# Twelve of sixteen gate blocks as seven half-size products in a hybrid attention layer

## The chip, the core and the metric

The kernel runs on one core of one Trainium2 chip. The metric is device time in microseconds. A time is that of a whole execution; the profile's span is the part of it between the first and the last instruction that the profiler records.

In the profile PE is TensorE's matmul row and PEld its weight loads, DVE is VectorE, ACT is ScalarE, POOL is GpSimd, SP is SyncE, whose queue here issues the loads of weights. ps and pt are the names of the eight PSUM banks, four of each.

## The reference

One layer with D = 1024 and 512 tokens, with 16 meta tokens in front: a SwiGLU FFN, a token mixer and a second SwiGLU FFN, each added to the residual.

```python
h = h + 0.5 * swiglu(rms_norm(h, ffn1_norm[l]), ffn1_w_in[l], ffn1_w_out[l])
h = h + token_mixer(rms_norm(h, mix_norm[l]), ...)
h = h + 0.5 * swiglu(rms_norm(h, ffn2_norm[l]), ffn2_w_in[l], ffn2_w_out[l])
```

The change is in the mixer's second half, behind the two attentions (fox with 8 heads, SWA with 8 query heads on 2 key heads):

```python
proj = h @ w_in                                   # q, k, v of both branches, and the gates ga, gb
y = jax.nn.sigmoid(ga) * (o_fox @ w_branch_fox) + jax.nn.sigmoid(gb) * (o_swa @ w_branch_swa)
return y @ w_out
```

ga and gb have 1024 features each, o_fox and o_swa 512, y and the result 1024.

## The kernel before

**Numbers and products.** All large products run in fp32r with both operands split into a high part (a rounded copy, made by `hi` on ScalarE) and a low part (the rest, made by `lo` on VectorE). `prod` (L279, L280, L282) issues three matmuls for each pair of 128x128 weights and moving columns: wh with xH, wh with xL, wl with xH. So every weight piece costs one cast on ScalarE (L130, tile wh) and one subtraction on VectorE (L137, tile wl).

**Weights.** They come in pieces in the fixed order of the list `pieces`. `piece()` hands out the next one, splits three pieces ahead and loads five ahead. raw, wh and wl have three buffers each. An instruction waits in its engine's queue for the ones before it; which order the instructions of an engine have is set by a scheduler when the kernel is built, from the data they need, and does not change at run time.

**Seven products for eight.** The FFNs take two weight blocks and two token halves as a 2x2 block product and form it from seven half-size products (`Units.seven`): pieces A, B, C and D hold the blocks b1 and b2 and sums of their halves, the moving side is x in quarters (A11, A12, A22) and four sums of quarters (S1 to S4). The weight sums are made partly by accumulating loads that POOL issues (`load_first`, `load_others`) and partly by VectorE (L221, L222). Each product is 12 matmuls of half the tokens. One unit is 84 matmuls. The product of S4 (`p3`) is left pending and runs inside the next unit.

**The mixer.** Features lie on partitions, tokens on columns. x~ is the residual times the norm's gain, not yet times each token's rms factor (rb1); its two parts xH and xL are kept in SBUF. The residual is written to DRAM as h1d. After the two attentions' projections, four lists of steps are woven: attention units in `main` and plain products in `fills`, so that TensorE has matmuls while VectorE and ScalarE do a unit's softmax. An SWA unit is scores, turn (transposes of the weights) and values. The eight blocks of ga are such fills: four beside the first SWA head group, four beside the second. `keep_gate` stores each, times rb1, in zA. The gate stage follows: for each of four pairs of features two blocks of gb (24 matmuls of 512 columns each, from xH and xL), the sigmoids, then four branch products (12 matmuls each) with the split outputs oH, oL, and y split into yH, yL. The output projection takes token halves of 256 and adds into h2T, which is loaded from h1d on ScalarE's queue (L1516). Weight pieces of it follow each other every 24 matmuls.

Of the kernel before, what the change touches and what calls it, by code (L numbers as in the profile page):

```python
# [24 lines left out]
M = 16  # L25
# [11 lines left out]
NU = DFF // P  # L37
NC = (4, 3)
TH = T // 2

# [39 lines left out]
def kernel(  # L80
# [108 lines left out]
    xm_place = lambda n: cp.tile([P, KD * P], F32R, tag="xm", name=nm(n))  # L189
    state = {"use": 0, "load": 0, "split": 0}  # L190
    shared = {}
# [35 lines left out]
    def load_to(n):  # L227
        while state["load"] < min(n, len(pieces)):
            c = state["load"]
# [913 lines left out]
    def normalise(parts):  # L1143

        l = new("l", [P, 4], F32, 2)[:, : len(parts)]
        for j, (t, nmx) in enumerate(parts):
            A.activation(t, t, AF.Exp, bias=nmx, scale=-1.0, accum_out=l[:, j : j + 1])  # L1147
# [226 lines left out]

    def feat_steps(wsrc, srcH, srcL, nk, c0, use, cuts=4, w=S):

        box = {}

        def part(j):
            if j == 0:  # L1380
                box["w"] = wsrc()
                box["ps"] = psum()
# [42 lines left out]
    def pre(p, ip):  # L1425
# [33 lines left out]
    run(main[0][:1] + fills[0][:2])  # L1459
    del main[0][:1], fills[0][:2]  # L1460
    for m, f in zip(main, fills):
        run(weave(m, f))
    stM.close()


    stG = ExitStack()
    gp = stG.enter_context(tc.tile_pool(name="gates", bufs=1))
    yH = gp.tile([P, KD, S], F32R, name="yH")
    yL = gp.tile([P, KD, S], F32R, name="yL")
    oH = gp.tile([P, 2, 4, S], F32R, name="oH")  # L1470
    oL = gp.tile([P, 2, 4, S], F32R, name="oL")

    for c in range(4):
        sA, sB = {}, {}

        def gate_b(m):
            def use(ps):
                z = gp.tile([P, S], F32, tag="gz", name=nm("gz"), bufs=3)
                V.tensor_tensor(out=z, in0=ps, in1=rb1, op=ALU.mult)
                sB[m] = gp.tile([P, S], F32, tag="sg", name=nm("sg"), bufs=3)  # L1480
                A.activation(sB[m], z, AF.Sigmoid)

            return use

        for m in range(2):
            run(feat_steps(piece, xH, xL, KD, M, gate_b(m)))
        for m in range(2):
            sA[m] = gp.tile([P, S], F32, tag="sa", name=nm("sa"), bufs=3)
            A.activation(sA[m], zA[:, 2 * c + m], AF.Sigmoid)
        if c == 0:  # L1490
            for b in range(2):
                for k in range(4):
                    hi(oH[:, b, k], oA[:, b, k])
                    lo(oL[:, b, k], oA[:, b, k], oH[:, b, k])
        wF, wS = piece(), piece()
        for m in range(2):
            mi = 2 * c + m
            cut = lambda w: tuple(t[:, :, m * P : m * P + P] for t in w)

            def use_f(ps):  # L1500
                V.tensor_tensor(out=sA[m], in0=sA[m], in1=ps, op=ALU.mult)

            def use_s(ps):
                s = sB[m]
                V.tensor_tensor(out=s, in0=s, in1=ps, op=ALU.mult)
                V.tensor_tensor(out=s, in0=s, in1=sA[m], op=ALU.add)
                hi(yH[:, mi], s)
                lo(yL[:, mi], s, yH[:, mi])

            run(feat_steps(lambda: cut(wF), oH[:, 0], oL[:, 0], 4, 0, use_f))  # L1510
            run(feat_steps(lambda: cut(wS), oH[:, 1], oL[:, 1], 4, 0, use_s))

# [6 lines left out]
    def add_out(mi, c):  # L1519
        def use(ps):  # L1520
# [4 lines left out]
            else:  # L1525
                sq = gp.tile([P, S], F32, tag="gz", name=nm("sq2"), bufs=3)[:, : S // 2]
                A.activation(sq, hv, AF.Square)
# [178 lines left out]
```

## Time and profile before

| | |
|---|---|
| median of 3 runs | 1094.58 us (1093.43 to 1096.65) |
| profiled execution | 1096.85 us, span 1095.1 us, TensorE clock 0.996 |
| busy share | PE 99%, PEld 95%, DVE 76%, ACT 55%, POOL 15% |
| SWA units and fills | about 540 to 612 us |
| gate stage | 612 to 700 us |
| output projection | 700 to 747 us |

The lines of groups give out<-in by the program's names with shapes, then busy time and mean duration in ns. In a timeline a row is start, duration (both us), engine, line, operation, and in brackets how long the engine had been idle and what released it. A duration of TensorE, VectorE or ScalarE can overlap the next one's start.

### The profile page before, as it was taken

Reading aid. Unit: us, or ns where it says so; the run is one execution under the profiler, and the core shown is the slowest. Engines: PE = TensorE matmul, PEld = TensorE weight load, DVE = VectorE, ACT = ScalarE, POOL = GpSimd, SP = SyncE. Lnnn points to the kernel's source line nnn. Section 1 sums busy time; section 2 is a strip of 40 time slices with the busy share of each in tenths; the row PEclk is TensorE's granted clock in tenths of the full one; section 3 lists DMA queues with packets and bytes.
Section 4 is the critical chain, followed back from the end, with each engine's and each line's share of the span. In section 5 each row is a group of like instructions: output and inputs, shape, how many; then the busy total and the mean of one; then the engine's idle time right before and its main releaser. Section 6 shows DMA issues by size and latency. Waiting matters only on the chain.

```text
span 1095.1 us, 21329 instructions
## 1 busy us (share of the span) xinstructions
PE 1084.8 (99%) x8317; PEld 1036.0 (95%) x8317; DVE 831.5 (76%) x1569; ACT 600.8 (55%) x1115; POOL 167.4 (15%) x201
## 2 busy tenths in 40 slices
PE   9999999999999999999999999999999999999998
PEld 8999999999999999999887888899999999999997
DVE  6868868988889587788787655678798778886653
ACT  6556446656666455466555533355476466645640
POOL 1011111121124431122100000000122211221000
PEclk8999999999999999999999999999999999999999
DMA  8467787688776323112211224456589777887522
GB/s 272 114 196 192 174 197 199 153 221 211 178 179 170 119 88 109 59 40 80 79 58 58 77 86 147 153 174 182 136 192 185 193 192 178 180 192 181 147 77 78
DMA packets 96693, 161.45 MB, mean 147 GB/s; under 512 B 10112, under 2 KB 46464, under 8 KB 96592
## 3 DMA queue, kind: packets, MB, share of 16 engines
q1 hardware_dynamic: 65520, 119.93, 34.4%
q0 software_dynamic: 22688, 29.44, 18.1%
q10 hardware_dynamic: 8384, 10.72, 3.1%
q8 instruction: 65, 1.06, 0.4%
q14 instruction: 36, 0.29, 0.1%
HBM read 155.84 MB, written 6.32 MB: 148 GB/s over the span
## 4 chain that ended last, share of the span: by engine, by line
PE 95%; DVE 2%; ACT 1%; DMA 0%; issue 0%; POOL 0%; SPq 0%; ACTq 0%
PE ps L279 16%; PE ps L280 16%; PE ps L282 16%; PE pt L279 13%; PE pt L280 13%; PE pt L282 13%; ACT t L1147 1%; PE pt L1232 0%; DMA xt<-in_x_dram 0%; DVE wl L137 0%; PE pt L1187 0%; PE ps L1354 0%; PE pt L1354 0%; PE ps L1187 0%; DVE t L1150 0%; PE pt L1247 0%
## 5 line engine op out<-in xcount | busy, mean ns | idle before, releaser
L279 PE MATMUL ps<-x,wh 128*128 128x264 f32 (+2 forms) x768 | 226.4, 295 | 1.5 <-ACT pt L500 1.5
L280 PE MATMUL ps<-x,wh 128*128 128x264 f32 (+2 forms) x768 | 225.7, 294 | 0.9 <-DVE x L137 0.6
L282 PE MATMUL ps<-x,wl 128*128 128x264 f32 (+2 forms) x768 | 225.4, 294 | 0.0
L137 DVE TENSOR_TENSOR wl<-raw,wh 128x1024 fp32r<-128x1024 f32 (+3 forms) x136 | 164.5, 1210 | 75.6 <-ACT wh L130 73.5
L130 ACT CAST wh<-raw 128x1024 fp32r<-128x1024 f32 (+3 forms) x136 | 140.7, 1036 | 142.1 <-PE ps L280 46.7
L279 PEld LDWEIGHTS ps<-x,wh 128*128 128x128 f32 x768 | 145.9, 190 | 4.7 <-ACT pt L500 1.7
L280 PEld LDWEIGHTS ps<-x,wh 128*128 128x128 f32 x768 | 145.6, 190 | 3.9 <-DVE x L137 0.8
L282 PEld LDWEIGHTS ps<-x,wl 128*128 128x128 f32 x768 | 145.8, 190 | 2.8
L279 PE MATMUL pt<-x,wh 128*128 128x264 f32 (+2 forms) x416 | 125.4, 301 | 0.0
L280 PE MATMUL pt<-x,wh 128*128 128x264 f32 (+2 forms) x416 | 124.8, 300 | 0.0
L282 PE MATMUL pt<-x,wl 128*128 128x264 f32 (+2 forms) x416 | 124.6, 300 | 0.0
L137 DVE TENSOR_TENSOR wl<-tc,wh 128x1024 fp32r<-128x1024 f32 (+1 forms) x57 | 68.7, 1204 | 32.7 <-ACT wh L130 32.4
L130 ACT CAST wh<-tc 128x1024 fp32r<-128x1024 f32 (+1 forms) x57 | 59.0, 1035 | 58.2 <-DVE tc L222 48.3
L279 PE MATMUL ps<-acts,wh 128*128 128x264 f32 (+1 forms) x304 | 86.5, 285 | 0.0
L282 PE MATMUL ps<-acts,wl 128*128 128x264 f32 (+1 forms) x304 | 86.2, 283 | 0.0
L280 PE MATMUL ps<-acts,wh 128*128 128x264 f32 (+1 forms) x304 | 86.0, 283 | 0.0
L279 PEld LDWEIGHTS pt<-x,wh 128*128 128x128 f32 x416 | 78.4, 188 | 2.9 <-issue 0.3
L282 PEld LDWEIGHTS pt<-x,wl 128*128 128x128 f32 x416 | 78.5, 189 | 2.8
L280 PEld LDWEIGHTS pt<-x,wh 128*128 128x128 f32 x416 | 78.2, 188 | 2.5
L137 DVE TENSOR_TENSOR wl<-rawC,wh 128x1024 fp32r<-128x1024 f32 (+1 forms) x57 | 69.4, 1218 | 5.3 <-ACT wh L130 5.0
L130 ACT CAST wh<-rawC 128x1024 fp32r<-128x1024 f32 (+1 forms) x57 | 58.9, 1033 | 22.2 <-PE pt L280 15.7
L279 PE MATMUL pt<-acts,wh 128*128 128x264 f32 (+1 forms) x208 | 59.2, 285 | 0.0
(382 smaller groups left out, 3046.6 us busy)
## 6 DMA issues: line engine op xcount, KB each, us to landing
rawC<-in_w2i_dram SPq DMA_DIRECT2D x19, 512.0 KB, 4.4
raw<-in_w2i_dram SPq DMA_DIRECT2D x38, 256.0 KB, 3.7
rawC<-in_w1i_dram SPq DMA_DIRECT2D x18, 512.0 KB, 4.4
raw<-in_w1i_dram SPq DMA_DIRECT2D x36, 256.0 KB, 3.4
raw<-in_wm_dram SPq DMA_DIRECT2D x18, 512.0 KB, 4.5
raw<-in_wg_dram SPq DMA_DIRECT2D x16, 512.0 KB, 3.3
raw<-in_wout_dram SPq DMA_DIRECT2D x16, 512.0 KB, 3.3
rawD<-in_w2i_dram SPq DMA_DIRECT2D x19, 256.0 KB, 4.0
```

The costliest lines, as they stand in the source:

```text
L130: return A.copy(o, i)
L137: return V.tensor_tensor(out=o, in0=i, in1=h, op=ALU.subtract)
L279: PE.matmul(ps, sH, mH, start=first, stop=False, **more)
L280: PE.matmul(ps, sH, mL, start=False, stop=False, **more)
L282: shared["mm"] = PE.matmul(ps, sL, mH, start=False, stop=last, **more)
L1147: A.activation(t, t, AF.Exp, bias=nmx, scale=-1.0, accum_out=l[:, j : j + 1])
```

## The change

Sixteen gate blocks were plain products. Now the blocks 0 to 3 of ga stay plain and the other twelve (4 to 7 of ga, 0 to 7 of gb) go in six pairs through `Units.seven`, with token halves of 256. The order of the work around them changes:

- The fills beside the first SWA group are three gate blocks in place of four; beside the second they are the eight fox branch products, whose split inputs are written into buffers that earlier attention parts held (`fox_parts`), and whose results ScalarE copies out.
- The fourth gate block and the eight SWA branch products run after the attentions. The high parts of the SWA output go into a part of xH and xL that is not read any more (`Unused`), once the first half of that gate's matmuls is done.
- x~ in fp32 is made again, from h1d: four loads of 512 KB on ScalarE's queue, eight scalings on ScalarE (L1573), and on VectorE four sums of quarters (L1580), each then split (S1 to S4).
- Then six units: two for ga, in which POOL multiplies each sigmoid into the fox product (zA), and four for gb, in which VectorE multiplies the sigmoid into the SWA product, POOL adds zA, and y is split in pieces of 256 columns.
- The loads of the first unit's pieces B to D are held back until the gate stage's pool is open.

```diff
-    for m in range(KD):
-        pieces.append(("w", [(wg[m], 8, 128)]))
-    for c in range(4):
-        pieces += [("w", [(wg[KD + 2 * c + m], 8, 128)]) for m in range(2)]
-        pieces += [("w", [(wbr[b, c], 4, 256)]) for b in range(2)]
+    pieces += [("w", [(wg[m], 8, 128)]) for m in range(NG - 1)]
+    pieces += [("w", [(wbr[0, c], 4, 256)]) for c in range(4)]
+    pieces.append(("w", [(wg[NG - 1], 8, 128)]))
+    pieces += [("w", [(wbr[1, c], 4, 256)]) for c in range(4)]
+
+    hold = len(pieces) + 1
+    for m in range(NG, 2 * KD, 2):
+        seven_pieces(wg[m], wg[m + 1], 4)
...
-    gates = [s for m in range(KD) for s in feat_steps(piece, xH, xL, KD, M, keep_gate(m))]
+    gates = [s for m in range(NG - 1) for s in feat_steps(piece, xH, xL, KD, M, keep_gate(m))]
...
+    def split_o(b, oh_, ol):
+        for k in range(4):
+            src, l = oA[:, b, k], ol[:, k]
+            if b:
+                src, l = (v.rearrange("p (a c) -> p a c", a=2) for v in (src, l))
+            hi(oh_[:, k], src)
+            lo(l, src, oh_[:, k])
+
+    def fox_parts():
+
+        oF["h"] = new("v", [P, NB + 1, 512])[:, :4]
+        oF["l"] = new("qH", [P, 4, S])
+        oF["f"] = [new("k" + x, [P, 2, KW]).rearrange("p a c -> p (a c)").bitcast(F32) for x in "HL"]
+        split_o(0, oF["h"], oF["l"])
...
-        qb1[4:-1] + gates[:LAG] + qb1[-1:] + gates[LAG : 2 * KD],
-        gates[2 * KD :],
+        qb1[4:-1] + gates[:LAG] + qb1[-1:] + gates[LAG:],
+        foxes,
...
+    for k in range(0, KD, 2):
+        A.dma_start(xg[:, k : k + 2], h1d[:, k : k + 2])
...
+    def last_gate(ps):
+        V.tensor_tensor(out=zl, in0=ps, in1=rb1, op=ALU.mult)
+        A.activation(zl, zl, AF.Sigmoid)
+        V.tensor_tensor(out=zA[:, NG - 1], in0=zA[:, NG - 1], in1=zl, op=ALU.mult)
+
+    steps = feat_steps(piece, xH, xL, KD, M, last_gate, whole=True)
+    run(steps[:2])
+    split_o(1, oW, oLs)
+    run(steps[2:])
+    for k in range(KD):
+        A.activation(xg[:, k], xg[:, k], AF.Identity, scale=gmT[:, k : k + 1])
...
+    sum_of(0, xq(0, 0), xq(1, 0))
+    parts_of(0, "S3")
+    sum_of(1, xq(1, 0), xq(1, 1))
+    sum_of(2, at[1], xq(0, 0))
+    parts_of(2, "S2")
+    parts_of(1, "S1")
+    sum_of(3, xq(0, 1), at[2], ALU.add)
+    parts_of(3, "S4")
...
+    for m in range(KD):
+        run(branch_steps(1, m, (oW, oLs), lambda ps, m=m: A.copy(swa_out(m), ps)))
...
+        def sigma(i, t, v, in_place):
+            z = v if in_place else small("gz", 2)
+            tt(z, v, rb1[:, halves[t]])
+            c, mi = halves[t], m + i
+            sg = small("sg", 2)
+            A.activation(sg, z, AF.Sigmoid)
+            if b:
+                s = swa_out(mi)[:, c]
+                tt(s, s, sg)
+                (V if mi == KD - 1 and not t else G).tensor_tensor(out=s, in0=s, in1=zA[:, mi, c], op=ALU.add)
+                hi(yH[:, mi, c], s)
+                lo(yL[:, mi, c], s, yH[:, mi, c])
+            else:
+                G.tensor_tensor(out=zA[:, mi, c], in0=zA[:, mi, c], in1=sg, op=ALU.mult)
...
+            if what == "P7":
+                box["p7"] = small("p7")
+                A.copy(box["p7"], ps)
...
+            elif what == "C21 - U2":
+                u2 = small("u2")
+                A.copy(u2, box["u2"])
+                tt(u2, ps, u2, ALU.add)
+                sigma(0, 1, u2, True)
+            elif what == "C11":
+                sigma(0, 0, ps, False)
+            elif what == "C22 + P7":
+                o = small("c22")
+                tt(o, ps, box["p7"], ALU.subtract)
+                sigma(1, 1, o, True)
+            else:
+                sigma(1, 0, ps, False)
...
+    for m in range(NG, KD, 2):
+        gg.seven(gate(m, 0), False, src)
+    for m in range(0, KD, 2):
+        gg.seven(gate(m, 1), m == KD - 2, src)
```

Three places in VectorE's order show it. The first is the entry into the gate stage. Before, from the last attention output (oA) on: the low parts of the attention outputs (oL) stand between the first gate's z (gz) and weight pieces (wl).

```order
L1061 TENSOR_TENSOR oA<-pt_8178,hsq_8188 64x2x128
L1398 TENSOR_TENSOR zA<-pt_8138,rb_4863 128x512
L137 TENSOR_TENSOR wl_8213<-raw_8028,wh_8212 128x1024
L137 TENSOR_TENSOR oL<-oA,oH 128x512 x4
L1479 TENSOR_TENSOR gz_8243<-ps_8218,rb_4863 128x512
L137 TENSOR_TENSOR oL<-oA,oH 128x512
L137 TENSOR_TENSOR wl_8248<-raw_8136,wh_8247 128x1024
```

Now (spare is the z of the last plain gate and then the place of the x~ sums, oLs the low parts of the SWA output, x_42.. its high parts, xg x~, S_1397 the sum S3, S_1389 S1, S_1398 S2, wl_8286 the third piece of the SWA branch):

```order
L1564 TENSOR_TENSOR spare<-pt_8229,rb_4863 128x512
L138 TENSOR_TENSOR oLs<-oA,x_4275 128x512
L138 TENSOR_TENSOR oLs<-oA,x_4276 128x512
L138 TENSOR_TENSOR oLs<-oA,x_4279 128x512
L138 TENSOR_TENSOR oLs<-oA,x_4280 128x512
L1566 TENSOR_TENSOR zA<-zA,spare 128x512
L1580 TENSOR_TENSOR spare<-xg 128x1024 x2
L138 TENSOR_TENSOR S_1397_8215<-spare,S_1397_8215 128x1024
L1580 TENSOR_TENSOR spare<-spare,xg 128x1024
L138 TENSOR_TENSOR S_1389_8203<-spare,S_1389_8203 128x1024
L1580 TENSOR_TENSOR spare<-xg,spare 128x1024
L138 TENSOR_TENSOR S_1398_8217<-spare,S_1398_8217 128x1024
```

The next row is L138's wl_8286: the weight piece stands behind the x~ sums and three of their low parts.

The second place is the middle of the stage. Before, one pair of features between two weight pieces (sa and sg the sigmoids of ga and gb, then the products):

```order
L1501 TENSOR_TENSOR sa_8594<-sa_8594,ps_8610 128x512
L1505 TENSOR_TENSOR sg_8557<-sg_8557,pt_8624 128x512
L1506 TENSOR_TENSOR sg_8557<-sg_8557,sa_8594 128x512
L137 TENSOR_TENSOR yL<-sg_8557,yH 128x512
L1501 TENSOR_TENSOR sa_8596<-sa_8596,ps_8641 128x512
L137 TENSOR_TENSOR wl_8605<-raw_8563,wh_8604 128x1024
```

Now, a part of the second unit of gb (oA holds the SWA product and becomes y, sg is the sigmoid, u and c the gate's z in place):

```order
L138 TENSOR_TENSOR wD_8903<-rawD_8753,wD_8903 128x512
L225 TENSOR_TENSOR tc_8992<-rawC_8906,rawD_8907 128x512
L1611 TENSOR_TENSOR oA<-oA,sg_8897 128x256
L1611 TENSOR_TENSOR u_1507_8937<-ps_8868,u_1507_8937 128x256
L226 TENSOR_TENSOR tc_8992<-tc_8992,rawC_8906 128x512
L138 TENSOR_TENSOR yL<-oA,yH 128x256
L1611 TENSOR_TENSOR u_1507_8937<-u_1507_8937,rb_4863 128x256
L1611 TENSOR_TENSOR gz_8963<-pt_8854,rb_4863 128x256
L138 TENSOR_TENSOR wl_8996<-tc_8992,wh_8995 128x1024
L1611 TENSOR_TENSOR oA<-oA,sg_8941 128x256
L1611 TENSOR_TENSOR oA<-oA,sg_8965 128x256
```

The operations on y are half as wide and twice as many, and weight sums and more splits stand between them.

The third place is the start of the output projection. Before, the sums into h2T and the splits of its weight pieces alternate:

```order
L137 TENSOR_TENSOR yL<-sg_8740,yH 128x512
L1522 TENSOR_TENSOR h2T<-h2T,ps_8837 128x256
L137 TENSOR_TENSOR wl_8865<-raw_8756,wh_8864 128x1024
L1522 TENSOR_TENSOR h2T<-h2T,pt_8870 128x256
L137 TENSOR_TENSOR wl_8900<-raw_8835,wh_8899 128x1024
```

Now (wl_9368 is the fourth piece of the output projection):

```order
L1625 TENSOR_TENSOR oA<-oA,zA 128x256
L138 TENSOR_TENSOR yL<-oA,yH 128x256
L1668 TENSOR_TENSOR h2T<-h2T,pt_9340 128x256
L1668 TENSOR_TENSOR h2T<-h2T,ps_9373 128x256
L1668 TENSOR_TENSOR h2T<-h2T,pt_9408 128x256
L138 TENSOR_TENSOR wl_9368<-raw_9297,wh_9367 128x1024
L1674 TENSOR_TENSOR sqacc<-sqacc,gz_9399 128x256
```

Three sums into h2T stand ahead of the piece.

More of the change, by code (lines that the diff above doesn't have):

```diff
@@ L38 @@
 NC = (4, 3)
+NG = 4
 TH = T // 2
@@ L189 @@
     xm_place = lambda n: cp.tile([P, KD * P], F32R, tag="xm", name=nm(n))
-    state = {"use": 0, "load": 0, "split": 0}
+    state = {"use": 0, "load": 0, "split": 0, "hold": hold}
     shared = {}
@@ L227, in load_to @@
     def load_to(n):
-        while state["load"] < min(n, len(pieces)):
+        while state["load"] < min(n, state.get("hold", n), len(pieces)):
             c = state["load"]
@@ L1460 @@
     del main[0][:1], fills[0][:2]
+    main[3].insert(0, fox_parts)
     for m, f in zip(main, fills):
         run(weave(m, f))
+    for m in range(NG - 1):
+        with after(shared["exp"]):
+            A.activation(zA[:, m], zA[:, m], AF.Sigmoid)
+        V.tensor_tensor(out=zA[:, m], in0=zA[:, m], in1=fox_out(m), op=ALU.mult)
     stM.close()
@@ L1467 @@
     gp = stG.enter_context(tc.tile_pool(name="gates", bufs=1))
[L1468 to L1511, printed above, removed]
@@ new lines @@
+    HF = S // 2
+    halves = (slice(0, HF), slice(HF, S))
+    shared["tp"] = gp
+    shared["wd"] = lambda: xm_place("wD")
+    banks["turn"] = None
+    spare = gp.tile([P, KD, S], F32, tag="yL", name="spare")
+    part = lambda name: gp.tile([P, 2, 4, HF], F32R, tag=name, name=nm(name))
+    small = lambda tag, bufs=1: gp.tile([P, HF], F32, tag=tag, name=nm(tag), bufs=bufs)
+    xS = {"S1": part("S1")}
+    oLs = gp.tile([P, 4, S], F32R, name="oLs")
+    for tag, n in (("p7", 1), ("gz", 2), ("sg", 2), ("u2", 1), ("c22", 1)):
+        for _ in range(n):
+            small(tag, n)
@@ new lines @@
+    gp.tile([P, PW], F32, tag="tc", name="tc", bufs=1)
+    for _ in range(2):
+        gp.tile([P, 512], F32, tag="rawD", name="rawD", bufs=2)
+    xS["S3"] = part("S3")
+    xg = gp.tile([P, KD, S], F32, tag="yH", name="xg")
+    for name in ("S2", "S4"):
+        xS[name] = part(name)
+    del state["hold"]
+    for k in range(0, KD, 2):
+        A.dma_start(xg[:, k : k + 2], h1d[:, k : k + 2])
+    zl = spare[:, KD - 1]
+    def last_gate(ps):
+        V.tensor_tensor(out=zl, in0=ps, in1=rb1, op=ALU.mult)
+        A.activation(zl, zl, AF.Sigmoid)
+        V.tensor_tensor(out=zA[:, NG - 1], in0=zA[:, NG - 1], in1=zl, op=ALU.mult)
```

58 lines of the change are left out of this document (54 added, 4 removed).

## The prediction, made before the result was known

> **What bounds the kernel now.** I read the page's first part, then the stretches of the stages that the change touches, then the single instructions there.
>
> ```profile
> PE 1084.8 (99%) x8317; PEld 1036.0 (95%) x8317; DVE 831.5 (76%) x1569; ACT 600.8 (55%) x1115; POOL 167.4 (15%) x201
> ...
> 612.00:700.00 88.00, 88.00 (x382) 71.64 (x381) 49.45 (x62) 33.37 (x47) 0.00 (x0) 1.00 0.35 114
> ...
> 700.00:747.00 47.00, 47.00 (x395) 46.81 (x394) 37.32 (x59) 24.29 (x34) 0.70 (x1) 1.00 0.54 180
> ...
> 800.00:850.00 50.00, 50.00 (x424) 49.96 (x423) 44.48 (x77) 32.00 (x58) 11.64 (x10) 1.00 0.89 196
> ```
>
> The columns of a stretch are its length, then busy time and instructions of PE, PEld, DVE, ACT and POOL. TensorE is never idle in the gate stage (612 to 700), in the output projection behind it, or in the second FFN's seven-product units. In the gate stage DVE is busy for 49 of 88 us and POOL does nothing; in the FFN units DVE is at 44 of 50. So the gate stage costs what its matmuls cost, and has room on DVE that seven-product units use up.
>
> A matmul's listed duration overlaps its neighbours; its cost is the distance between starts.
>
> ```profile
> L279 PE MATMUL ps<-oH,wh x32: 389/389/401, 622.3 to 696.6; 128*128 128x512 f32 x32
> ...
> 806.62 0.28 PE L279 MATMUL pt<-x,wD 128*128 128x256 f32 x1
> ...
> 816.55 0.28 PE L279 MATMUL pt<-x,wD 128*128 128x256 f32 x1
> ```
>
> The first row's first and last instruction are 321 matmuls apart in program order: 74.3 / 321 = 0.2315 us for one of 512 columns. The other two are the same place in two successive units, 84 matmuls of 256 columns: 9.93 us, 0.118 each.
>
> **The change, part by part.**
>
> *Fewer columns.* A pair of gate blocks takes 2 x 24 = 48 matmuls of 512 columns, 11.11 us; as a unit it takes 9.93. Six pairs: 6 x 1.18 = **-7.1 us**. The branch products keep their 192 matmuls; four gates stay plain. SWA's second head group keeps its fill (96 matmuls of branch product for 96 of gates); the first gives up 24, which run later and alone. The shortest cover left between scores and their transposes there is 18 matmuls, 4.2 us, as in pieces of the order before, where TensorE never waited: 0, at worst +1.
>
> *The DVE's price list.*
>
> ```profile
> 800.06 0.68 DVE L137 TENSOR_TENSOR wD<-rawD,wD 128x512 fp32r<-128x512 f32 x1
> 800.66 0.42 DVE L794 TENSOR_TENSOR sums<-u,sums 128x256 f32<-128x256 f32 x1
> ...
> 801.59 0.42 DVE L137 TENSOR_TENSOR acts<-sums,acts 128x256 fp32r<-128x256 f32 x1
> 801.93 0.42 DVE L537 TENSOR_TENSOR u<-ps,u 128x256 f32<-128x256 f32 x1
> 802.26 0.68 DVE L221 TENSOR_TENSOR tc<-rawC,rawD 128x512 f32<-128x512 f32 x1
> 802.98 0.69 DVE L222 TENSOR_TENSOR tc<-tc,rawC 128x512 f32<-128x512 f32 x1
> ...
> 804.87 1.22 DVE L137 TENSOR_TENSOR wl<-tc,wh 128x1024 fp32r<-128x1024 f32 x1
> 806.01 1.22 DVE L137 TENSOR_TENSOR wl<-rawC,wh 128x1024 fp32r<-128x1024 f32 x1
> ...
> 816.79 0.43 DVE L794 TENSOR_TENSOR sums<-u,u 128x256 f32<-128x256 f32 x1
> 817.25 0.43 DVE L794 TENSOR_TENSOR sums<-sums,u 128x256 f32<-128x256 f32 x1
> ```
>
> Start to start: 1024 columns 1.14 us, 512 columns 0.60, 256 columns 0.335; behind an operation that makes its input 0.72 and 0.46.
>
> *Entry of the stage.* DVE now makes the kept gate's z (0.60) before the four low parts of the SWA output. TensorE's second branch matmul needs the first of them, about 0.60 + 0.68 + hand-over = 1.4 us after the gate product ends; the four matmuls that the order puts ahead cover 0.9. **+0.6** (0.4 to 2, the far end if ScalarE's casts come late, below).
>
> *x~ again.* Four loads of 512 KB, eight scalings, four sums, four splits.
>
> ```profile
> 803.76 1.05 ACT L130 CAST wh<-tc 128x1024 fp32r<-128x1024 f32 x1 [0.69 <-DVE tc L222]
> 804.72 1.04 ACT L130 CAST wh<-rawC 128x1024 fp32r<-128x1024 f32 x1
> ...
> 673.99 0.62 ACT L130 CAST yH<-sg 128x512 fp32r<-128x512 f32 x1 [5.63 <-DVE sg L1506]
> 674.52 0.63 ACT L1489 ACTIVATE sa<-zA 128x512 f32<-128x512 f32 x1
> ...
> 675.18 1.30 ACTq L1516 DMA_DIRECT2D h2T<-h1d  x3
> ...
> 683.45 1.05 ACT L130 CAST wh<-raw 128x1024 fp32r<-128x1024 f32 x1 [3.26 <-DMA h2T<-h1d]
> GB/s 289 0 0 295 55 0 44 317 0 0 45 229 310 298 280 193 333 356 274 134 0 115 235 0 0 0 0 259 87 186 178 104 251 300 71 320 49 314 66 284
> ```
>
> On ScalarE 1024 columns take 0.96, 512 columns 0.53 and a load's issue 0.43; such a row of loads once held ScalarE for 3.3 us. Behind the four issues there stand the casts of the SWA output, which the branch products need. With t = 0 at the start of the kept gate's product: issues until about 3, casts to 5 (7 if it is held), sigmoid, eight scalings: 11 to 12. The data come in time: 2 MB here and up to 2 MB of weights on the other queue at some 290 GB/s (the last row, slices of 1.5 us, 676 to 690) are 7 to 14 us. From the second sum DVE has seven operations of 1024 columns, the last of them the third branch piece's wl: 12 + 8.0 = 20. TensorE wants that wl after 24 + 48 + 8 matmuls, 18.5 + 0.5 = 19. **+1.0**; 0 if ScalarE isn't held, +5 if the loads land 4 us later.
>
> *DVE in the units.* A unit of the first gates costs DVE three splits of 1024 (3.42), one of 512 (0.60), two sums (1.32), six operations of 256 and two dependences (2.25): 7.6 us of 9.93. A unit of the second gates has eight more of 256 (four products with the sigmoid, four low parts of y): 10.3, that is 0.35 more than TensorE needs. And POOL, idle here before, gets four operations of 256 columns in each unit. What one does to DVE, from the end of FFN 1:
>
> ```profile
> 342.45 1.65 POOL L863 TENSOR_TENSOR sqacc<-sqacc,u 128x528 f32<-128x528 f32 x1
> 347.64 1.85 POOL L863 TENSOR_TENSOR sqacc<-sqacc,u 128x528 f32<-128x528 f32 x1
> 352.67 1.57 POOL L863 TENSOR_TENSOR sqacc<-sqacc,u 128x528 f32<-128x528 f32 x1 [0.50 <-ACT u L862]
> 356.60 1.89 POOL L863 TENSOR_TENSOR sqacc<-sqacc,u 128x528 f32<-128x528 f32 x1 [0.26 <-ACT u L862]
> 363.24 1.34 POOL L863 TENSOR_TENSOR sqacc<-sqacc,u 128x528 f32<-128x528 f32 x1
> ...
> 342.58 2.09 DVE L139 SCALAR_TENSOR_TENSOR x<-hT,gT,x 128x528 fp32r<-128x528 f32 x1
> 347.54 0.76 DVE L139 SCALAR_TENSOR_TENSOR x<-hT,gT,x 128x528 fp32r<-128x528 f32 x1
> 353.32 1.49 DVE L139 SCALAR_TENSOR_TENSOR x<-hT,gT,x 128x528 fp32r<-128x528 f32 x1
> 357.43 2.14 DVE L137 TENSOR_TENSOR wl<-rawC,wh 128x1024 fp32r<-128x1024 f32 x1
> ```
>
> DVE operations that read two tiles in SBUF took 2.09 and 1.49 in place of 0.76, and 2.14 in place of 1.22, while POOL worked: 3.0 us lost over the five of POOL, whose free length is 1.34, so 45% of it. At 256 columns POOL takes about 1.34 x 256 / 528 = 0.65 and costs DVE 0.3; four make 1.2. The second gates' units ask 11.5 us of DVE for 9.93 of TensorE, and four of them leave it 6.0 late. It enters with a lead: a piece's buffer is free 2.85 us into a unit and refilled (0.96 on ScalarE, 1.14 on DVE) for a use 7.1 us later, 5 us. So 1 us of waiting in the last unit. Then y: without a lead DVE still has up to three splits for the output projection (3.4) and the last blocks' operations (a chain of z, sigmoid, product, sum, cast, low part, some 2.7) when TensorE has only 36 matmuls without the last two blocks, 4.2 us: about 3. **+4.1**; 0 if POOL always falls beside reads of PSUM (10.3 x 4 stays inside the lead), +10 if each of its operations holds DVE for the whole 0.65 (12.9 a unit, 11.8 late, 6.8 in the units and 3 at the end).
>
> The Trainium skill's "SBUF — State Buffer", section "Who interferes with whom", says that a DVE instruction with two SBUF inputs contends with a GpSimd instruction that reads SBUF, by an exclusive lock, and that the loser waits for the whole instruction. The trace agrees that it can (2.09 us at 342.58); by that rule taken at its worst the sum is that of the second rival below.
>
> *Output projection.* The h2T loads wait for zA, which is now read until the last add, and three h2T sums stand ahead of the fourth weight piece's wl on DVE. The third sum waits for the third block's product: 0.42 + 1.14 behind it, less the two matmuls that need only wh. **+1.5** (1.3 to 3.5, as these loads took 4.7 us to land).
>
> ```profile
> h2T<-h1d ACTq DMA_DIRECT2D x8, 256.0 KB, 4.7
> ```
>
> **Sum.** -7.1 + 0.6 + 1.0 + 4.1 + 1.5 = +0.1 us. The profiled execution had a span of 1095.1 and a time of 1096.85; the runs' median is 1094.58, and a difference carries over. Forecast: **1095 us, no change that can be told**; a measurement of this kernel tells a change from about 0.3%, 3.3 us. Its own range is 1091.5 to 1098.
>
> **The rivals.**
>
> *It keeps most of the gain.* POOL's operations fall beside DVE's reads of PSUM or its waits, so that the units and the end cost nothing, and x~ is ready in time: -7.1 + 0.4 + 0 + 0 + 1.4 = -5.3, 1089.3. For it: the FFN units run with DVE at 89% and no gap, and one of POOL's operations above (beside 347.54) cost DVE nothing. Against it: DVE's own 10.3 us exceed 9.93 with no POOL at all. Chance 0.29.
>
> *POOL holds DVE.* Every operation of POOL stops DVE's next one for its length. It decides once the excess of a unit passes 5 / 4 = 1.25 us, which is 0.9 of hold. The sum is -7.1 + 0.6 + 1.0 + 10 + 1.5 = +6.0, 1100.6. For it: three of five holds seen. Against: four of DVE's fourteen small operations read PSUM, and POOL too has to wait for DVE. Chance 0.16.
>
> *x~ comes late.* The loads share the queues with the first units' weights and their accumulating halves, and land 4 us later: 1.0 becomes 5, the sum +4.1, 1098.7. For it: ScalarE's 3.26 us wait for loads of this kind. Against: 356 GB/s in that same place. Chance 0.09.
>
> That the units are not done, or that 256-column matmuls cost more than half, is excluded by the order of TensorE's instructions and by the 395 matmuls in 47 us.
>
> **How the numbers follow.** Forecast 0.46. Faster is the first rival, 0.29; slower the other two, 0.25; the forecast's own range lies within the 0.3%. The range that holds the time 8 times in 10 reaches to both sides' cases: 1089 to 1100.5.
>
> **What would show it.** Right or wrong in the profile after: matmuls of 256 columns in the gate units at 0.118 us (else the gain is off); TensorE's idle time before the products with oLs and with the third branch piece, under 0.6 and 1.0 us; DVE above 90% busy in the last four units, with operations of 1024 columns that take well over 1.22 us beside POOL's; idle time of TensorE before the first products with yH of 2 to 4 us, and of 1 to 2 before the fourth output block. If DVE shows waits and no long operations there, the term of POOL is wrong; if TensorE waits for x~ sums (S3, S2) or DMA, the loads are.

## The result and the profile after

The changed kernel takes **1106.56 us** (median of 4, 1105.06 to 1108.36) where the kernel before took 1094.01 beside it: a ratio of 1.0114, 95% interval 1.01 to 1.0127. It is 12.5 us slower. The forecast was 1095 with no change that can be told, and its range ended at 1100.5.

The first part of the page of the changed kernel:

```profile
PE 1082.1 (98%) x8533; PEld 1041.4 (94%) x8533; DVE 862.7 (78%) x1630; ACT 636.8 (58%) x1199; POOL 200.4 (18%) x236
```

Of its span of 1104.2 us TensorE is idle for 22.1, where it was idle for 10.3 of 1095.1. The stretches of the stages from 622 us on (columns as in the prediction, then the granted clock, the share of the DMA engines and GB/s), of the changed kernel:

```profile
622.00:632.00 10.00, 6.32 (x18) 3.93 (x17) 10.00 (x10) 8.80 (x12) 0.00 (x0) 0.77 0.27 59
632.00:662.00 30.00, 30.00 (x210) 27.97 (x210) 20.61 (x29) 15.75 (x27) 11.04 (x13) 0.96 0.74 185
662.00:712.00 50.00, 43.39 (x356) 42.15 (x354) 46.39 (x78) 29.86 (x64) 19.26 (x20) 1.00 0.39 107
712.00:758.00 46.00, 43.58 (x363) 43.06 (x364) 34.60 (x59) 23.74 (x35) 0.71 (x1) 1.00 0.65 206
```

Three stretches lose time: SWA's branch products (622 to 632), where the granted clock is 0.77 as well, the units (662 to 712), with VectorE busy for 46.4 of 50 us, and the output projection. What TensorE waited for between 600 and 735 (behind the arrow stands what ended the wait; columns: us in total, times, longest):

```profile
PE pt L283 <- DVE c L1611: 3.8, 2, 2.4
PE pt L283 <- ACT oA L1600: 3.7, 3, 1.8
PE ps L283 <- ACT p L1634: 2.3, 3, 1.5
PE ps L286 <- DVE wl L138: 1.9, 1, 1.9
PE pt L283 <- ACT x L131: 1.0, 1, 1.0
PE pt L283 <- ACT yH L131: 0.9, 1, 0.9
PE pt L1370 <- DVE pL L138: 0.4, 1, 0.4
```

Lines of the changed kernel are 4 higher in the helpers: L131 is the high part, L138 the low part. L1600 copies SWA's branch product out of PSUM, L1634 the product P7, L1611 works on the gates' results ("c" is C22).

I set each term of the prediction's sum against the distance between TensorE's starts, less the 0.2315 us of a matmul of 512 columns or the 0.118 of one of 256:

| step | predicted | in the trace |
|---|---|---|
| fewer columns | -7.1 | -7.1 (run x9 below) |
| end of the attention part | 0 | 0.85 |
| entry of the stage | 0.6 | 1.2 |
| x~ again | 1.0 | 5.2, and 2.2 of half clock behind it |
| units and end of y | 4.1 | 6.9 and 1.0 |
| output projection | 1.5 | 2.4 |
| sum | +0.1 | +12.65 |

The last matmul of the output projection, first before, then in the changed kernel, starts 11.95 us later:

```profile
746.80 0.28 PE L282 MATMUL pt<-yH,wl 128*128 128x256 f32 x1
```

```profile
758.75 0.28 PE L286 MATMUL ps<-yH,wl 128*128 128x256 f32 x1
```

These two times can't be compared as they stand. The profiled execution of before had lost 1.5 us at its start: it had half the clock from 11.7 to 18.5, where the changed kernel's had all of it. The last matmul that both kernels make in the same place ahead of the change starts at 531.95 before and at 530.47 now. From it to the end of the output projection it is 214.85 us before and 228.28 now, 13.4 more. The sum accounts for 12.65 of that; the rest is gaps of about 0.1 us that the table leaves out.

The spans differ by 9.1 only, because the profiled execution of before also waits in the second FFN, which the changed kernel's does not. Its longest wait there:

```profile
787.18 0.39 PE L279 MATMUL ps<-x,wh 128*128 128x256 f32 x1 [1.48 <-ACT pt L500]
```

That execution took 1096.85 us, 2.8 above the median. So stages are compared below by the time from that common matmul to the last one of the output projection ("stage"), and kernels by their ratio to before.

The entry and x~ have one cause that the trace shows on ScalarE. Its instructions in the changed kernel, from the entry of the stage:

```profile
605.48 0.82 ACTq L1558 DMA_DIRECT2D xg<-h1d  x2
...
606.35 4.82 ACTq L1558 DMA_DIRECT2D xg<-h1d  x2
611.21 2.18 ACT L131 CAST x<-oA 128x512 fp32r<-128x512 f32 x4 [4.57 <-PE pt L286]
...
613.83 3.77 ACT L1573 ACTIVATE xg<-xg,gT 128x512 f32<-128x512 f32 x6
620.40 1.34 ACT L1573 ACTIVATE xg<-xg,gT 128x512 f32<-128x512 f32 x2 [2.80 <-DMA xg<-h1d]
621.64 1.04 ACT L131 CAST S<-spare 128x1024 fp32r<-128x1024 f32 x1
622.59 1.04 ACT L131 CAST wh<-raw 128x1024 fp32r<-128x1024 f32 x1
...
624.48 1.06 ACT L1600 COPY oA<-pt 128x512 f32<-128x512 f32 x2
```

The row of 4.82 us covers the third and the fourth issue of x~ loads, but an issue is short: the four take 0.33 to 0.46 us each. Between the third and the fourth ScalarE's queue stands still for 4.05 us. The chain that ended last (start and length) shows why:

```profile
605.48 5.34 DMA xg<-h1d
...
610.84 9.54 DMA xg<-h1d
```

The first load lands at 610.82, and the fourth is issued at 610.84. In the trace the fourth counts its landing on the same semaphore as the first, and waits for that one ahead of its issue. The SWA casts stand behind it and start at 611.21; the bracket there names TensorE, whose product had let the same casts start at 606.34 and 607.68 in x1_sp below. The last two scalings wait 2.80 us more for the data of that fourth load, and behind them stand the weight cast for the third branch piece and the copies that empty the PSUM banks. TensorE's answer is this:

```profile
622.89 0.39 PE L286 MATMUL pt<-x,wl 128*128 128x512 f32 x1
625.10 0.51 PE L283 MATMUL pt<-x,wh 128*128 128x512 f32 x1 [1.83 <-ACT oA L1600]
...
627.96 0.80 PE L283 MATMUL pt<-x,wh 128*128 128x512 f32 x1 [1.64 <-ACT oA L1600]
...
631.27 0.63 PE L284 MATMUL pt<-oLs,wh 128*128 128x512 f32 x1
631.70 0.63 PE L286 MATMUL pt<-x,wl 128*128 128x512 f32 x1
```

The last two rows wait for nothing and start 0.43 us apart in place of 0.2315: half the clock, from about 627.5 to 634.3.

### The profile page after: what moved, and what is told of

Read it like the earlier page. It is cut to its first block, busy times and chain, and to the rows that moved or that the text cites. A ratio compares the mean times of both kernels' runs of the same rounds, so it can differ in the third digit from the quotient of the medians.

```text
span 1104.2 us, 22059 instructions
## 1 busy us (share of the span) xinstructions
PE 1082.1 (98%) x8533; PEld 1041.4 (94%) x8533; DVE 862.7 (78%) x1630; ACT 636.8 (58%) x1199; POOL 200.4 (18%) x236
## 4 chain that ended last, share of the span: by engine, by line
PE 86%; DVE 5%; ACT 4%; DMA 2%; issue 1%; POOL 1%; ACTq 0%; SPq 0%; DVEq 0%; POOLq 0%
PE ps L283 15%; PE ps L284 14%; PE ps L286 14%; PE pt L283 12%; PE pt L284 12%; PE pt L286 12%; DVE wl L138 2%; DMA xg<-h1d 1%; ACT wh L131 1%; ACT t L1151 1%; POOL oA L1625 1%; PE pt L1236 1%; PE pt L1191 0%; DMA xt<-in_x_dram 0%; DMA h2T<-h1d 0%
## 5 line engine op out<-in xcount | busy, mean ns | idle before, releaser
L283 PE MATMUL ps<-x,wh 128*128 128x256 f32 (+2 forms) x768 | 220.0, 287 | 2.4 <-ACT p L1634 2.3
L284 PE MATMUL ps<-x,wh 128*128 128x256 f32 (+2 forms) x768 | 219.2, 286 | 0.6 <-DVE x L140 0.4
L286 PE MATMUL ps<-x,wl 128*128 128x256 f32 (+2 forms) x768 | 218.8, 285 | 0.0
L138 DVE TENSOR_TENSOR wl<-raw,wh 128x1024 fp32r<-128x1024 f32 (+3 forms) x130 | 157.7, 1214 | 71.9 <-ACT wh L131 71.1
L131 ACT CAST wh<-raw 128x1024 fp32r<-128x1024 f32 (+3 forms) x130 | 134.4, 1036 | 109.1 <-PE ps L284 51.7
L283 PE MATMUL pt<-x,wh 128*128 128x256 f32 (+2 forms) x424 | 126.8, 300 | 4.7 <-ACT oA L1600 3.7
L286 PE MATMUL pt<-x,wl 128*128 128x256 f32 (+2 forms) x424 | 125.3, 297 | 0.0
L284 PE MATMUL pt<-x,wh 128*128 128x256 f32 (+2 forms) x392 | 112.7, 288 | 0.0
L138 DVE TENSOR_TENSOR wl<-tc,wh 128x1024 fp32r<-128x1024 f32 (+1 forms) x63 | 75.9, 1205 | 37.8 <-ACT wh L131 37.4
L131 ACT CAST wh<-tc 128x1024 fp32r<-128x1024 f32 (+1 forms) x63 | 65.3, 1036 | 62.9 <-DVE tc L226 52.4
L138 DVE TENSOR_TENSOR wl<-rawC,wh 128x1024 fp32r<-128x1024 f32 (+1 forms) x63 | 78.1, 1239 | 7.9 <-ACT wh L131 7.6
L131 ACT CAST wh<-rawC 128x1024 fp32r<-128x1024 f32 (+1 forms) x63 | 65.2, 1034 | 25.7 <-PE pt L284 17.2
```

What stands on the lines that cost most here:

```text
L131: return A.copy(o, i)
L138: return V.tensor_tensor(out=o, in0=i, in1=h, op=ALU.subtract)
L283: PE.matmul(ps, sH, mH, start=first, stop=False, **more)
L284: PE.matmul(ps, sH, mL, start=False, stop=False, **more)
L286: shared["mm"] = PE.matmul(ps, sL, mH, start=False, stop=last, **more)
```

## The experiments

Each kernel is the changed kernel, or the run that its heading or expectation names, with the edit shown. The stage is the time in us from the common matmul to the last one of the output projection; it is 214.85 before and 228.28 in the changed kernel. It is read from one execution of each kernel, so it differs from what the ratios give by up to 1.4 us. The first seven rows of the table stand against a median of before of 1093.3 to 1093.4, the last three against 1093.78.

| run | median us | ratio to before, interval | stage |
|---|---|---|---|
| x1_sp | 1096.54 | 1.0034 [1.0018, 1.005] | 218.49 |
| x2_banks | 1106.02 | 1.0117 [1.0102, 1.0132] | 228.19 |
| x3_no_xt | 1099.02 | 1.0054 [1.0034, 1.0073] | 221.63 |
| x4_no_pool | 1098.04 | 1.0044 [1.0029, 1.0059] | 220.03 |
| x5_sp_dve | 1097.83 | 1.0041 [1.0028, 1.0053] | 220.12 |
| x6_pool_loads | 1097.54 | 1.0045 [1.0032, 1.0058] | 219.71 |
| x7_end | 1090.34 | 0.9976 [0.9965, 0.9986] | 212.31 |
| x8_sp_end | 1094.13 | 1.0004 [0.9995, 1.0013] | 216.03 |
| x9_floor | 1087.27 | 0.9939 [0.9926, 0.9951] | 209.11 |
| x10_mix | 1092.25 | 0.9987 [0.9978, 0.9995] | 214.85 |

### x1_sp: x~ on SyncE's queue, ahead of the units' weights

```diff
-    del state["hold"]
     for k in range(0, KD, 2):
-        A.dma_start(xg[:, k : k + 2], h1d[:, k : k + 2])
+        SP.dma_start(xg[:, k : k + 2], h1d[:, k : k + 2])
+    del state["hold"]
```

> The four x~ loads stand on SyncE's queue, ahead of the units' weights, in place of ScalarE's. Everything else is as in the changed kernel. Theory L (late x~): the loads shared the DMA engines with the units' weights and held ScalarE for 5.3 us (605.48 to 610.84), so the casts of the SWA output came 1.2 us late, the scalings and, behind them in ScalarE's order, the copies of the branch results 5.2 us late, and the clock fell to half for 2.2 us behind that. With the loads first in one queue, ScalarE is not held: casts by about 607, all of x~ by about 614, and most of these 8.6 us go: about 1099. Rival B (the four PSUM banks): TensorE waits because eight branch blocks have only four banks, whenever ScalarE has twelve other operations to do in that stage; then only the 1.2 us and part of the rest go: 1103 to 1105.

The stage is 9.8 us shorter. TensorE has no gap over 0.12 us between 602 and 666: the 1.2, the 5.2 and the 2.2 us are gone. The SWA casts come at 606.34 and 607.68, and the loads land in 6.4 us in place of 8.2: here each has a semaphore of its own, all four are issued within 1.8 us, and the last has landed by 613.3. Two microseconds at the end of y and the output projection went too, and a new 1.5 us of half clock at 699 came. Theory L fits; the next runs tell what in it counts.

### x2_banks: eight PSUM banks

```diff
+    banks["turn"] = False
     for m in range(KD):
         run(branch_steps(1, m, (oW, oLs), lambda ps, m=m: A.copy(swa_out(m), ps)))
+    banks["turn"] = None
```

> The eight blocks of SWA's branch product alternate over all eight PSUM banks in place of four; loads and order are as in the changed kernel. Rival B (the four banks): no block waits for a copy out of PSUM any more, the 5.2 us of waits between 622 and 630 and the 2.2 us of half clock behind them go, the 1.2 us at the casts stay: about 1099. Theory L (late x~): the copies are late all the same, the units find the sums, the weights' casts and the branch results late, and the time stays above 1103.

No gain. TensorE no longer waits for a copy, and in that place its waits are these (between 600 and 735):

```profile
PE pt L283 <- ACT wh L131: 1.9, 1, 1.9
...
PE pt L286 <- DVE wl L138: 1.2, 1, 1.2
PE pt L283 <- ACT x L131: 1.2, 1, 1.2
```

It goes on to the next branch piece and finds its weights not split, since that cast stands behind the same scalings; the half clock follows (629.6 to 636.4) as before. Rival B falls. The wait that a profile names is the first of several that end at nearly the same time.

### x3_no_xt: no x~ at all

```diff
-    for k in range(0, KD, 2):
-        A.dma_start(xg[:, k : k + 2], h1d[:, k : k + 2])
...
-    for k in range(KD):
-        A.activation(xg[:, k], xg[:, k], AF.Identity, scale=gmT[:, k : k + 1])
...
-    xq = lambda tok, feat: xg[:, 4 * feat : 4 * feat + 4, halves[tok]]
+    xq = lambda tok, feat: zA[:, 4 * feat : 4 * feat + 4, halves[tok]]
```

> Leaves out the four x~ loads and the eight scalings; the sums read other data of the same shape, so the output is not the reference's. Theory L: without them nothing holds ScalarE, 8.6 us go: 1098, and TensorE has no gap over 0.3 us between 600 and 635 but the one before the kept gate. Rival B: 5 of the 8.6 us stay, 1103. This is the floor for what x1_sp and x2_banks can reach.

No gap over 0.12 us from 602 to 655, as Theory L said; the time is a microsecond above the 1098 expected. It is not below x1_sp, as a floor would be: its units wait 7.8 us (x1_sp 6.3), and it has half clock twice, at 672 and 703. The order of ScalarE's and VectorE's work in the units had changed with what was left out.

### x6_pool_loads: the loads issued by POOL

```diff
-        A.dma_start(xg[:, k : k + 2], h1d[:, k : k + 2])
+        G.dma_start(xg[:, k : k + 2], h1d[:, k : k + 2])
```

> The changed kernel with the four x~ loads issued by POOL, so that they hold no operation of ScalarE, while they still share the DMA engines with the first units' weights. If the 8.6 us came from ScalarE being held at the issue (5.3 us at 605.48), they go: 1098. If they came from the data landing late beside 4 MB of weights, only the 1.2 us at the SWA casts go: 1104 to 1105.

ScalarE's rows of this run:

```profile
606.30 1.15 ACT L131 CAST x<-oA 128x512 fp32r<-128x512 f32 x2
...
614.85 1.03 ACT L131 CAST wh<-raw 128x1024 fp32r<-128x1024 f32 x1
...
618.69 1.34 ACT L1573 ACTIVATE xg<-xg,gT 128x512 f32<-128x512 f32 x2 [0.75 <-DMA xg<-h1d]
```

The data land nearly as late as in the changed kernel: the last two scalings start at 618.69, there at 620.40. Beside the units' weights the last load lands 5.3 us later than in x1_sp, where it goes first. Yet of the 8.6 us of waits and half clock only 0.5 is left, and the stage is 8.6 us shorter. So late data alone cost next to nothing; they cost through what stands behind them on ScalarE. Two things changed there together: no issue stands still ahead of the casts (on POOL each load has a semaphore of its own), and the weight cast (614.85, there 622.59) now stands ahead of the last scalings. This run doesn't separate the two, and the loads on ScalarE with four semaphores were not tried.

### x4_no_pool: without POOL's operations in the gates

```diff
-                (V if mi == KD - 1 and not t else G).tensor_tensor(out=s, in0=s, in1=zA[:, mi, c], op=ALU.add)
+                if mi == KD - 1 and not t:
+                    V.tensor_tensor(out=s, in0=s, in1=zA[:, mi, c], op=ALU.add)
...
-                G.tensor_tensor(out=zA[:, mi, c], in0=zA[:, mi, c], in1=sg, op=ALU.mult)
+                pass
```

> Leaves out the 23 operations of POOL in the gate stage (the product with the first sigmoid, the add of the second gates), so the output is not the reference's; VectorE, ScalarE and TensorE keep all of theirs. Theory H (POOL holds VectorE and the casts of y wait for POOL's add): the waits of the units and of the end, some 8 us in all, fall to 2: 1100 to 1101. Rival C (VectorE has not the capacity: its own 10.3 us for TensorE's 9.93, with hand-overs, and single buffers): at most 2 us go, 1104 to 1105, and VectorE stays over 95% busy from 662 to 702.

The stage is 8.3 us shorter, and TensorE's waits in the units and at y fall from 7.9 us to 0.4. VectorE alone, at 10.3 us for TensorE's 9.93, keeps up, so rival C falls in the form that it has here. What POOL does to VectorE, in groups of instructions between 640 and 705 (busy us, mean ns), first in the changed kernel, then without POOL's operations:

```profile
L138 DVE TENSOR_TENSOR wl<-rawC,wh 128x1024 fp32r<-128x1024 f32 x6 | 8.7, 1458 | 2.7 <-ACT wh L131 2.7
...
L1611 DVE TENSOR_TENSOR u<-u,rb 128x256 f32<-128x256 f32 x6 | 5.5, 916 | 0.1
...
L1611 DVE TENSOR_TENSOR gz<-pt,rb 128x256 f32<-128x256 f32 x10 | 4.2, 416 | 0.1
```

```profile
L138 DVE TENSOR_TENSOR wl<-rawC,wh 128x1024 fp32r<-128x1024 f32 x6 | 7.3, 1222 | 2.8 <-ACT wh L131 2.7
...
L1611 DVE TENSOR_TENSOR gz<-pt,rb 128x256 f32<-128x256 f32 x12 | 5.0, 419 | 0.1
...
L1611 DVE TENSOR_TENSOR u<-u,rb 128x256 f32<-128x256 f32 x6 | 2.5, 423 | 0.1
```

The operation with both inputs in SBUF goes from 423 to 916 ns, the one that reads PSUM stays at 416. Over all groups the excess is 7.9 us for POOL's 20 operations there, 0.4 each. The prediction took 0.3. So the price on VectorE was about right; x8_sp_end below looks for what else made the wait.

### x5_sp_dve: x1_sp, and POOL's operations on VectorE

```diff
-                (V if mi == KD - 1 and not t else G).tensor_tensor(out=s, in0=s, in1=zA[:, mi, c], op=ALU.add)
+                V.tensor_tensor(out=s, in0=s, in1=zA[:, mi, c], op=ALU.add)
...
-                G.tensor_tensor(out=zA[:, mi, c], in0=zA[:, mi, c], in1=sg, op=ALU.mult)
+                V.tensor_tensor(out=zA[:, mi, c], in0=zA[:, mi, c], in1=sg, op=ALU.mult)
```

> x1_sp, and POOL's operations of the gate stage on VectorE (the product with the first sigmoid, the add of the second gates), where each takes 0.335 us. Measured so far: x1_sp 1096.5, and 8.5 us less without POOL's operations. If POOL holds VectorE for its whole operation (0.72 us and more, theory H), taking them over is cheaper for VectorE itself: 10.3 + 4 x 0.335 = 11.6 us a unit, 1.7 x 4 = 6.9 late, less a lead of 5, so 2 us of waits and 1 to 2 at the end: 1090 to 1092. If it holds it for 45% (the prediction's value, 0.3 us at 256 columns), nothing changes: 1096 to 1097. If VectorE's own work is the limit (rival C), it is slower: 1098 or more.

The time of x1_sp, as the 45% case said, but by two effects that cancel. The units' waits fall from 6.3 us to 2.3. At the output projection TensorE now waits 3.1 us for a wh and 2.4 for a wl, with some 3 us of half clock behind them. VectorE's rows there show why:

```profile
706.12 0.42 DVE L1666 TENSOR_TENSOR h2T<-h2T,pt 128x256 f32<-128x256 f32 x1 [3.58 <-DMA h2T<-h1d]
...
709.15 0.42 DVE L1666 TENSOR_TENSOR h2T<-h2T,pt 128x256 f32<-128x256 f32 x1 [0.25 <-DMA h2T<-h1d]
709.49 1.22 DVE L138 TENSOR_TENSOR wl<-raw,wh 128x1024 fp32r<-128x1024 f32 x1
```

The sums wait for the residual, whose loads could start only when zA was free, and the weight split stands behind all three. The wh waits for them too: on ScalarE its cast (706.90) stands behind the square of the first sum (706.58).

### x7_end: x5_sp_dve with the output projection mended

```diff
-    h2T = kp.tile([P, KD, S], F32, tag="z", name="h2T")
+    h2T = zA
...
-            V.tensor_tensor(out=hv, in0=hv, in1=ps, op=ALU.add)
+            with tc.issue_after(shared["lo"]):
+                V.tensor_tensor(out=hv, in0=hv, in1=ps, op=ALU.add)
```

> x5_sp_dve, and at the output projection: the eight loads of the residual go into the place of zA, each as soon as the last add has read its part, and each sum of the first blocks stands on VectorE behind the weight split that was emitted ahead of it. The wait ahead of the fourth block (1.4 us in x1_sp) and VectorE's waits for the loads go: 1.4 to 2 us under x5_sp_dve, so 1088 to 1090 if theory H is right. If the fourth piece is late because VectorE as a whole is late, the wait moves ahead to the first products with y and the time is that of x5_sp_dve.

A ratio of 0.9976 [0.9965, 0.9986]: this beats the kernel before, by 2.6 us, and the changed one by about 15 by the two ratios. More went than the 1.4 to 2 us expected: the stage is 7.8 us shorter than in x5_sp_dve, by the waits of 5.6 and the half clock that they brought. TensorE in this run, the units and the output projection:

```profile
662.00:702.00 40.00, 37.52 (x309) 36.57 (x308) 39.37 (x87) 25.98 (x56) 0.86 (x1) 1.00 0.45 128
702.00:743.00 41.00, 41.00 (x349) 40.96 (x348) 33.89 (x56) 22.82 (x32) 0.71 (x1) 1.00 0.62 204
```

VectorE is busy for 39.4 of 40 us in the units, where TensorE waits 3.2 in all (2.0 in the units, 1.2 at the first products with y). With 11.6 us a unit the prediction's own way of counting gives 4 x 1.7 - 5 = 1.8 in the units, which fits a lead of 5 us. The two edits were not tried apart.

### x8_sp_end: the same with POOL

x1_sp with the two edits of x7_end; the 23 operations stay on POOL.

> x1_sp with x7_end's edits at the output projection, and POOL's operations left on POOL; against x7_end it differs in nothing but who does those 23 operations. x1_sp waits 1.4 us ahead of the fourth block and loses 1.5 us more to half the clock at 699 to 702. Theory P (a POOL operation costs VectorE as much as doing it would, 0.38 us measured by VectorE's longer operations against 0.335): as x7_end, 1090 to 1092. Theory A (what costs with POOL is the way over ScalarE: it waits for each add ahead of its cast of y, 16 us in all, and the copy of P7 stands behind it): the waits of the units, 6.3 us in x1_sp, stay, and it is slower than x7_end by 2 to 4 us: 1093 to 1095.

The stage is 3.7 us longer than in x7_end; by the ratios it is 0.28% or 3.1 us. VectorE's load is about the same in both (busy for 862.6 us of the span here and for 861.0 in x7_end), so Theory P falls as the whole answer, and Theory A fits: of TensorE's waits here 2.6 us name the copy of P7, and only 0.9 an operation of VectorE. Its path, as the changed kernel shows it, first on POOL, then on ScalarE, then on TensorE:

```profile
674.16 2.51 POOL L1625 TENSOR_TENSOR oA<-oA,zA 128x256 f32<-128x256 f32 x2 [2.19 <-DVE oA L1611]
```

```profile
675.04 0.41 ACT L131 CAST yH<-oA 128x256 fp32r<-128x256 f32 x1 [0.76 <-POOL oA L1625]
676.71 0.41 ACT L131 CAST yH<-oA 128x256 fp32r<-128x256 f32 x1 [1.26 <-POOL oA L1625]
677.02 0.36 ACT L1634 COPY p<-ps 128x256 f32<-128x256 f32 x1
```

```profile
677.44 0.39 PE L283 MATMUL ps<-x,wh 128*128 128x256 f32 x1 [1.54 <-ACT p L1634]
```

Two adds take 2.51 us, while VectorE splits weights; ScalarE waits for each; the copy of P7, whose row names no wait of its own, stands behind the second cast until 677.02, and the next product needs its bank.

### x9_floor: what is left when nothing is late

```diff
-                V.tensor_tensor(out=s, in0=s, in1=zA[:, mi, c], op=ALU.add)
+                if mi == KD - 1:
+                    V.tensor_tensor(out=s, in0=s, in1=zA[:, mi, c], op=ALU.add)
...
-                V.tensor_tensor(out=zA[:, mi, c], in0=zA[:, mi, c], in1=sg, op=ALU.mult)
+                pass
```

> x7_end without 22 of the 24 products and adds (the product with the first sigmoid, the add of the second gates), so the output is not the reference's; one block keeps its adds. It shows what is left of the gain of 7.1 us when neither x~, nor VectorE's load, nor the output projection costs anything. If the sum's gain is right: before less 7.1, plus the 0.85 at the end of the attention part: 1087. If 1089 or more, the gain itself is smaller than worked out; x7_end then has almost all of it.

0.9939, or 6.7 us under before. TensorE waits 0.85 us at the end of the attention part and about 0.4 at y. The stage ends at this row and is 5.7 us shorter than before:

```profile
739.86 0.28 PE L286 MATMUL ps<-yH,wl 128*128 128x256 f32 x1
```

With those two waits that makes 7.0: the gain of 7.1 us is real. x7_end, 2.5 us shorter than before, keeps more than a third of it.

### x10_mix: the first gates' products on POOL

```diff
-                V.tensor_tensor(out=zA[:, mi, c], in0=zA[:, mi, c], in1=sg, op=ALU.mult)
+                G.tensor_tensor(out=zA[:, mi, c], in0=zA[:, mi, c], in1=sg, op=ALU.mult)
```

> x7_end with the eight products of the first gates back on POOL, in units that ask 7.6 us of VectorE for 9.93, and the adds of the second gates on VectorE. Theory P: those units have room, so holds there cost nothing, and VectorE enters the second gates with more lead: 0 to 1.5 us under x7_end, 1089 to 1090. If POOL's operations do cost there, 1091 or more.

The stage is 2.5 us longer than in x7_end; by the ratios it is 0.11%, and their intervals overlap. A miss: I had thought that those units have room. TensorE waits 0.5 us for the copy of P7 and 3.1 for weights, and loses some 1 us at half clock. Why more is lost than POOL's holds of 8 x 0.4 us can explain was not pursued.

## Why the prediction was wrong

**Fewer columns, -7.1: right.** x9_floor brings it out.

**The end of the attention part, 0, at worst +1: in its bound.** 0.85 us, in every run, where the last low parts of P have too little to cover them.

**Entry, +0.6: the step that failed is "0.6 (0.4 to 2, the far end if ScalarE's casts come late)".** The term itself, VectorE's z ahead of the low parts, costs nothing: in x1_sp, with the same z in the same place, TensorE doesn't wait. The 1.2 us are ScalarE's: its casts start at 611.21, in x1_sp at 606.34. That is the condition that I had named and given to the far end.

**x~ again, +1.0 (0 to 5): the largest error.** With the clock it cost 7.4. The step that failed is the schedule "issues until about 3, casts to 5 (7 if it is held) ... 11 to 12". ScalarE was held for 5.3 us, not 2, because the fourth load's issue waited until the first had landed, and it waited 2.8 more for data that "come in time": its scalings ended 16.6 us after the start of the kept gate's product (605.14), not 11 to 12. I had followed that lateness through VectorE alone, to the third piece's wl. On ScalarE itself the wh of that piece and the copies out of PSUM stand behind the same scalings, and the prediction doesn't name them. The rival "x~ comes late" had the place and the direction, and at 5 us most of the size. Its loads that share the queues and land late were there (5.3 us between x6_pool_loads and x1_sp), but as the cause they fall short: x6_pool_loads, with the last data at 618.7, loses 0.5 us. That its 5 us came near the 5.2 of waits is in part luck.

**The units, +4.1 (0 to 10): a wrong mechanism beside a good price.** A hold of 0.3 us was measured as 0.4; VectorE's 10.3 us and the lead of 5 us fit x4_no_pool and x7_end. (Its 11.5 us a unit leave VectorE 6.3 late after four, not 6.0; that changes little.) What failed is the step that let an operation on POOL cost only what it takes from VectorE. POOL's result goes on over ScalarE, whose order is fixed, and TensorE's PSUM bank waits at the end of that chain: 3 to 4 us by x8_sp_end against x7_end. The Trainium skill's "SBUF — State Buffer", section "Who interferes with whom", on which the second rival rested, agrees with the trace: the instruction with two SBUF inputs is held (423 to 916 ns), the one with an input in PSUM is not (419 and 416), and POOL is held as well (2.51 us for two adds, where one alone takes 0.73). That VectorE loses the whole length of POOL's operation is not borne out: its 0.65 for each is refuted by the 0.4. That this rival's 10 us came nearest to the 7.9 that TensorE waited is luck.

**The output projection, +1.5 (1.3 to 3.5): right in place and order, short by 0.9 us.** The three sums do stand ahead of the fourth piece's wl. But the third waits for its load, not for its product: it starts at 719.65 after 1.67 us for h2T<-h1d, the case of the range's far end. x7_end removes it.

**Half clock: not in the sum at all,** 2.2 us behind the waits for x~.

The two slower rivals were priced one at a time, at 1098.7 and 1100.6. Both mechanisms' waits came, at 7.4 and 7.9 us, and the range of single cases didn't hold their sum: with both at their rival's price it would have been +10, 1104.6. The half clock, 2.2 us, is about the rest.

## What to carry to other kernels

Before moving loads or a chain's link to an engine that looks idle or half used, write down that engine's instructions in order and ask what stands behind the one that waits: an issue that waits 4 us for an earlier load, or a 1 us add on POOL, costs what the copies behind it make TensorE wait. A wait that the profile names is the first of several that may be equally late, so widen one resource alone only as a test. A long row of merged issues can hide a wait: look at the single ones and at the critical chain. And when two late mechanisms sit in different stages, the range should hold their sum.

## What the runs showed of the hardware that was not expected

**The clock fell without a long pause.** The kernel before has a granted clock of 1.00 from 612 to 850. In the changed kernel it is half of that from about 627.5 to 634.3, behind six microseconds in which TensorE was busy for 2.5 us and no two starts were more than 2.2 us apart. It lasted 6.8 us there. In x10_mix it took less, pauses of at most 0.8 us, and half the clock lasted 3.4 us; its stretches:

```profile
676.00:680.00 4.00, 2.73 (x15) 2.11 (x15) 3.67 (x7) 4.00 (x7) 0.00 (x0) 0.90 0.04 15
680.00:684.00 4.00, 4.00 (x26) 4.00 (x25) 3.37 (x7) 1.10 (x4) 0.00 (x0) 0.67 0.32 77
```

In the changed kernel a longer pause, 2.57 us at 705, brought nothing:

```profile
704.00:712.00 8.00, 5.08 (x41) 4.67 (x40) 7.23 (x15) 4.32 (x10) 2.94 (x4) 1.00 0.36 116
```

So the longest pause doesn't decide it. The Trainium skill's "TensorE: Matmul & The Clock Gate", section "Part 1: The HAM clock gate", gives an idle window of about 3.4 us as the condition for half the clock, in windows that run free of the kernel's work. The half rate agrees (0.43 us between starts); pauses of 0.8 to 2.2 us between matmuls were enough here, which that condition alone doesn't tell. What share of a window has to be idle is open. For the sum it means that where it came, it cost another 1 to 3 us in these runs.

**What held ScalarE at the loads was a wait, not the issuing.** The four issues of 512 KB took 0.33 to 0.46 us each, but the fourth shared its semaphore with the first and stood until that one had landed, from 606.79 to 610.84. With four semaphores SyncE had issued the same loads after 1.8 us (x1_sp) and POOL after 2.2 (x6_pool_loads). x2_banks, with the loads as in the changed kernel, shows the wait again: the first load lands at 612.51, and the fourth is issued at 612.53.
